# Copying two low-rank products out of their banks, and a later due time for one stage of a chain

## The chip, the core and the metric

The kernel runs on one core of one Trainium2 chip. The metric is the device time of one execution in microseconds. A core has a matrix engine (TensorE, PE in the profile, with its weight loads as PEld), VectorE (DVE), ScalarE (ACT), GpSimd (POOL) and SyncE (SP), which here issues most transfers. TensorE writes its results to PSUM, eight banks; the other engines read them there.

## The reference

One decoder block on 272 tokens (16 meta tokens and 256 of the sequence) with a model width of 2048, all in float32:

```
xn = rms(h, n1);  proj = xn @ w_in                 # 2048 x (3520 + 3088 + 4096)
z_rwkv, z_fox, z_gate = split(proj)
z_rwkv = z_rwkv + (shift(z_rwkv) - z_rwkv) * mu    # token shift
r, k, v, wd, ad, gd = split(z_rwkv)                # 3 x 1024, and low rank 96, 96, 256
decay = exp(-exp(-softplus(-(w0 + tanh(wd) @ w2)) - 0.5))
a = sigmoid(a0 + ad @ a2);  g = sigmoid(gd) @ g2
y_a = groupnorm(wkv7_scan(r, decay, k', v, -kk, kk * a)) + bonus, times g   # 16 heads of 64
y_b = fox(z_fox)                                   # attention with a forget gate, 16 heads of 64
merged = sigmoid(gate_a) * (y_a @ w_a) + sigmoid(gate_b) * (y_b @ w_b)
h = h + merged @ w_o
out = h + (silu(gate) * up) @ w_dn                 # gate, up = split(rms(h, n2) @ w_gu), 5632 wide
```

The scan is a recurrence over tokens for each head.

## The kernel before

**Arithmetic.** Every float32 operand of a large product is split into a high part (a ScalarE copy to a rounded type) and a low part (VectorE subtracts the high part). A weight block is 128 x 1024: `wload` (L304 and on) brings `raw` in over SP's queue, ScalarE makes `wh` (L336), VectorE makes `wl` (L337), and TensorE does three products for one (`mm3`, L346 to L349). `raw`, `wh` and `wl` have four buffers each.

**Order of the work.** First come the low-rank products (`lora_jobs`): eight jobs that add up four banks, `lo0` to `lo3`. `lo0` (96 rows, called `pw`) and `lo1` (112 rows, called `pa`: 96 of the second product and 16 of the forget gate) lie in two of the four `main` banks, the two others in `aux` banks. Then for each of four groups g of four heads: `rwkv_jobs(g)` with the products k, v, r (four jobs each, two banks each) and the second low-rank stage (`g`, `sig`, `aa`), `fox_jobs(g)` with q, k, v of the attention (`f`), and two gate jobs (`zg`). The main banks go round, so the first `v` block takes the banks of `lo0` and `lo1` after the first `k` block took the two others. Branch products (`br`), the output product (`wo`) and the FFN (`gt`, `up`, `dn`) follow.

**Background stages.** Small work runs as generators, the streams, between the blocks of large products. A stream yields the planner nanoseconds until its next stage is due. `slot(ns)` is called after the two or three matmuls that a large product makes from one weight tile, with 3n/2.4 for n columns; it moves a planner clock on and starts at most one due stage, or a pair of a "fox" stage and a "chain" stage that together need at most four aux banks. After a stage the clock must pass MIX times the stage's own TensorE time, at least GAP, before the next one. A fox stage waits for a chain stage up to HOLD, 3500. TensorE's order is written out by hand in this way (`manual_schedule` on TensorE); the other engines' and the queues' orders are set when the program is built, by a planner that lets work go when its model has it ready.

**The streams the change touches.** `token_scales` is spawned by the last low-rank job with a delay of SCALES, 2500. It runs the rms matmuls, the root on VectorE (`rsb`, L263 to L272), and then `lora_post`, which reads the products in `lerp` (L468 for `lo0` and `lo1`, L471 for `lo2` and `lo3`) and in L572, where the forget gate's rows of `pa` are read. Its temporaries come from a ring of six tiles (`zt_`, ZB = 6).

`rwkv_bg(g)` is the scan of a group in chunks of 64 tokens. It builds scaled operands (`ar`, `bk`, one buffer each, L751 to L763), the matrices `NK` (`mat`, L786), and the inverse of a unit triangular matrix for each chunk: 32 x 32 blocks are inverted by 31 steps on VectorE (L874, L876), the results go through DRAM into `X` (L881 to L888), and the last blocks of X are made by two small products. The first, `QT` (32 matmuls of 32 x 32), is copied out by ScalarE (L962, two copies); the second, called X12 in the code and shown as X<-X,QT, reads the copies, is copied to X (L970), and the chain of chunks follows (`rhs`, `u`, `s`, `y`, copies L906, L920, L940 to L944). The first step of that chain, for the meta tokens, is interleaved: its `rhs` goes with the stage before QT, its `u` with QT, its `s` with X12. The lines around it:

```
        for h in range(2):
            nc.scalar.activation(QT[dn(h)].rearrange("p i s -> p (i s)"), ps[dn(h), 0:256], AF.Copy)
        next(meta_steps)
        yield Y_QT, ("chain", 2)
        ps = aux_ps(f"X12{g}")
```

This chain of group g runs while the k, v, r blocks of group g + 1 pass on TensorE; for the last group the gate jobs pass.

Of the kernel before, what the change touches and what calls it, by code (L numbers as in the profile page):

```python
# [12 lines left out]
AF = mybir.ActivationFunctionType  # L13
# [10 lines left out]
L = NMETA + T  # L24
# [66 lines left out]
Y_RHS = 1400  # L91
Y_U = 1400
Y_XT = 1400
Y_QT = 1200
Y_GN = 1400
FORGET = 14000
SCALES = 2500
# [3 lines left out]
def hybrid_block(ctx, tc, A, out, dbg=None):  # L101
    nc = tc.nc
# [17 lines left out]
    def aux_ps(name):  # L120
        return psa.tile([P, 512], F32, tag="aux", name=name)
# [12 lines left out]
    for h in range(2):  # L134
        rows = slice(h * HD, (h + 1) * HD)
# [73 lines left out]
    def zt_(name):  # L209
        return rw.tile([P, 274], F32, tag="z", name=name, bufs=ZB)  # L210
# [5 lines left out]
    def vc(name, i=0):  # L216
        c = COLS[name] + i
        return vcol[:, c:c + 1]
# [4 lines left out]
    def xload(i):  # L223
        xs[i] = et(f"xs{i}")
        nc.sync.dma_start(xs[i], A["hT"][:, 2 * i:2 * i + 2, :])
# [16 lines left out]
    def xsplit(i, m):  # L242

        k = 2 * i + m
        src, sc = (xs[i][:, m, :], vc("n1", k)) if k > 0 else (x0[:, :L], x0[:, L:])
        nc.scalar.activation(xh[:, k, :], src, AF.Copy, scale=sc)
        nc.vector.scalar_tensor_tensor(xl[:, k, :], src, sc, xh[:, k, :].bitcast(F32),
                                       op0=ALU.mult, op1=ALU.subtract)

    def squares(i):  # L250

        if i == 0:
            for m, src in enumerate((x0[:, :L], xs[0][:, 1, :])):
                nc.scalar.activation(xsum[:, m, :], src, AF.Square)
            return
        nc.scalar.activation(xs[i], xs[i], AF.Square)
        nc.vector.tensor_tensor(xsum, xsum, xs[i], op=ALU.add)
# [21 lines left out]
    def rstd1():  # L279
        parts = [et(f"{n}1").bitcast(F32R) for n in ("xqh", "xql")]  # L280
        split(*parts, xsum)

        def back():
            ps = aux_ps("rms1")[:, :L]
            for i in range(4):
                nc.tensor.matmul(ps, allones, parts[i % 2][:, i // 2, :], start=i == 0, stop=i == 3)
            ms = zt_("ms1")[:, :L]
            nc.vector.tensor_scalar(ms, ps, 1.0 / D, RMS_EPS, op0=ALU.mult, op1=ALU.add)
            nc.vector.tensor_scalar(epsw, ms, RMS_EPS, None, op0=ALU.mult)
            rt = zt_("rt1")[:, :L]  # L290
            rsqrt_small(None, rsb, ms, rt, None)
        return back
# [53 lines left out]
    def mm3(ps, wh, wl, ah, al, first, last):  # L346
        nc.tensor.matmul(ps, wh, ah, start=first, stop=False)  # L347
        nc.tensor.matmul(ps, wh, al, start=False, stop=False)  # L348
        nc.tensor.matmul(ps, wl, ah, start=False, stop=last)  # L349
# [8 lines left out]
    def spawn(gen, delay):  # L358
        streams.append([clock[0] + delay, gen, None])
# [148 lines left out]
    def lora_jobs():  # L508
        box = []

        def mk(q):
            def load():
                raw = raw0 if q == 0 else wp.tile([P, 1024], F32, tag="raw", name="raw", bufs=RAWB)
                wh = wp.tile([P, WCOLS], F32R, tag="wh", name="wh", bufs=WB)
                wl = wp.tile([P, WCOLS], F32R, tag="wl", name="wl", bufs=WB)
                if q > 0:
                    nc.sync.dma_start(raw[:, :2 * NLO], A["lora"][q])
                if 0 < q < 7:
                    xload(q + 1)
                for k in range(2):  # L520
                    cs = slice(k * NLO, (k + 1) * NLO)
                    if q == 0 and k == 0:
                        nc.vector.tensor_copy(wh[:, cs], raw[:, cs])
                    xsplit(q, k)
                    if q > 0 or k > 0:
                        nc.scalar.activation(wh[:, cs], raw[:, cs], AF.Copy)
                    nc.vector.tensor_tensor(wl[:, cs], raw[:, cs], wh[:, cs].bitcast(F32), op=ALU.subtract)
                squares(q)
                return [t[:, :2 * NLO].rearrange("p (k c) -> p k c", k=2) for t in (wh, wl)]

            def mul(w):
                if q == 0:
                    box.extend((main_ps if i < 2 else aux_ps)(f"lo{i}") for i in range(4))
                pw, pa, pg0, pg1 = box[:4]
                wh, wl = w
                outs = ((pw, 0, 96, 0, L), (pa, 96, 112, 0, L), (pg0, 208, P, 14, T + 2), (pg1, 208 + P, P, 14, T + 2))
                for k in range(2):
                    kt = q * 2 + k
                    if q == 0:

                        for i, (w_, x_) in enumerate(((wh, xh), (wh, xl), (wl, xh))):
                            for ps, c0, m, n0, n in outs:
                                nc.tensor.matmul(ps[:m, :n], w_[:, k, c0:c0 + m], x_[:, kt, n0:n0 + n],
                                                 start=kt == 0 and i == 0, stop=False)
                        continue
                    for ps, c0, m, n0, n in outs:
                        mm3(ps[:m, :n], wh[:, k, c0:c0 + m], wl[:, k, c0:c0 + m],
                            xh[:, kt, n0:n0 + n], xl[:, kt, n0:n0 + n], False, kt == KT - 1)
                if q == 6:
                    box.append(rstd1())  # L550
                if q == 7:
                    nc.vector.tensor_scalar(qk8, vc("q_g"), vc("k_g"), HD ** -0.5, op0=ALU.mult, op1=ALU.mult)
                    spawn(token_scales(*box), SCALES)
            return load, mul
        return [mk(q) for q in range(8)]

    def token_scales(pw, pa, pg0, pg1, back):
        back()
        lora_post(pw, pa, pg0, pg1)
        spawn(forget_gate(), FORGET)  # L560
        return
        yield

    def lora_post(pw, pa, pg0, pg1):
        tw = zt_("tw")
        lerp(pw, 96, vc("mu_w")[:96], tw[:96, :L], True)
        nc.scalar.activation(tw[:96, :L], tw[:96, :L], AF.Tanh)
        split(twh, twl, tw[:96, :L])
        ad = zt_("ad")
        lerp(pa, 96, vc("mu_a")[:96], ad[:96, :L], True)  # L570
        split(adh, adl, ad[:96, :L])
        nc.vector.tensor_tensor(fl[flr, :], pa[flr, :L], rsb[flr], op=ALU.mult)  # L572
        nc.vector.tensor_scalar(fl[flr, :], fl[flr, :], vc("mu_a")[flr], None, op0=ALU.add)
        for i, pg in enumerate((pg0, pg1)):
            sg = zt_("sg")
            lerp(pg, P, vc("mu_g", i), sg[:, :T], False)
            nc.scalar.activation(sg[:, :T], sg[:, :T], AF.Sigmoid)
            split(sgh[:, i, :], sgl[:, i, :], sg[:, :T])
# [135 lines left out]
    def rwkv_bg(g, box):  # L714
# [248 lines left out]
# [3 lines that stand above are left out]
# [477 lines left out]
```

## Time and profile before

| | us |
|---|---|
| median of 3 runs | 1539.01 |
| lowest and highest | 1537.67 and 1539.15 |
| the profiled execution | 1540.85 |
| its span, from the first to the last instruction | 1539.1 |
| PE busy in the span | 1529.6 (99%) |
| DVE busy | 1030.4 (67%) |
| ACT busy | 778.2 (51%) |
| POOL busy | 106.8 (7%) |

The profile is of one execution. A row of a timeline gives the start and the duration in us, the engine, the line of the kernel, the operation, what is written and read, and, in brackets, the idle time of the engine before it with what ended it. A row of a wait says which engine waited at which line for which work: us in total, times, the longest. A stretch gives each engine's busy us, the number of instructions, the granted clock of TensorE (1.00 is full speed), the DMA engines' share and GB/s. Ends of matmuls are modelled and they overlap, so what counts is the distance from start to start.

### The profile page before, as it was taken

The page shows a single profiled execution, that of the slowest core. Times are in us where ns is not written, and L with a number is a line of the kernel's source. Part 1 is how long each engine was busy: PE and PEld are TensorE (multiplying, and loading weights), DVE is VectorE, ACT ScalarE, POOL GpSimd, SP SyncE. Part 2 cuts the span into 40 slices and gives each one's busy share as a digit, 9 for nine tenths or more (in the row PEclk, how much of TensorE's full clock was granted, in tenths as well). Part 3 has the DMA queues.
Part 4 walks back from the last instruction along what each step waited for, and adds up shares of the span by engine and source line. Part 5 has one row for each costly group of instructions (what it writes and reads, how often), then busy time and mean ns, then how long its engine had stood idle before and what let it go on. Part 6 is the DMA issues. An engine that isn't in the chain of part 4 may idle for free.

```text
span 1539.1 us, 25987 instructions
## 1 busy us (share of the span) xinstructions
PE 1529.6 (99%) x10113; PEld 1352.5 (88%) x10113; DVE 1030.4 (67%) x1859; ACT 778.2 (51%) x1174; POOL 106.8 (7%) x186
## 2 busy tenths in 40 slices
PE   9999999999999999999999999999999999999998
PEld 9999899989989888998888888888888888888887
DVE  7887698688788857876565566666556666444443
ACT  7654465475465445554455455445445544333332
POOL 2111203302202000000000000000000000000000
PEclk9999999999999999999999999999999999999999
DMA  8566546546645757777566666666666665566663
GB/s 269 163 171 185 148 134 188 163 119 188 175 125 154 212 155 218 230 226 240 181 180 185 192 185 186 191 192 182 189 191 191 182 190 189 191 204 204 189 203 104
DMA packets 211483, 283.32 MB, mean 184 GB/s; under 512 B 23888, under 2 KB 128352, under 8 KB 211360
## 3 DMA queue, kind: packets, MB, share of 16 engines
q1 hardware_dynamic: 206752, 277.53, 60.7%
q10 hardware_dynamic: 4608, 4.13, 0.8%
q8 instruction: 79, 1.29, 0.3%
q14 instruction: 44, 0.36, 0.1%
HBM read 274.43 MB, written 7.19 MB: 183 GB/s over the span
## 4 chain that ended last, share of the span: by engine, by line
PE 95%; DVE 2%; ACT 1%; DMA 1%; SPq 1%; issue 1%; DVEq 0%; ACTq 0%
PE up L423 11%; PE gt L423 10%; PE zg L423 8%; PE dn L1306 5%; PE dn L1305 5%; PE dn L1304 5%; PE up L425 5%; PE gt L425 5%; PE zg L425 4%; PE f L347 2%; PE f L349 2%; PE f L348 2%; PE br L347 2%; PE f L423 2%; PE br L348 2%; PE br L349 2%
## 5 line engine op out<-in xcount | busy, mean ns | idle before, releaser
L337 DVE TENSOR_TENSOR wl<-raw,wh 128x1024 fp32r<-128x1024 f32 (+1 forms) x376 | 456.7, 1216 | 264.0 <-ACT wh L336 263.4
L336 ACT ACTIVATE wh<-raw 128x1024 fp32r<-128x1024 f32 (+1 forms) x376 | 393.9, 1049 | 424.8 <-PE up L423 117.5
L318 DVE TENSOR_TENSOR wl<-raw,wh 128x1024 fp32r<-128x1024 f32 x120 | 147.0, 1225 | 162.8 <-ACT wh L317 162.7
L423 PE MATMUL gt<-hts,wh 128*128 128x512 f32 x704 | 245.0, 394 | 0.0
L423 PE MATMUL up<-hts,wh 128*128 128x512 f32 x704 | 244.9, 394 | 0.0
L317 ACT ACTIVATE wh<-raw 128x1024 fp32r<-128x1024 f32 x120 | 127.0, 1058 | 194.4 <-PE dn L1305 141.5
L425 PE MATMUL gt<-hts,wl 128*128 128x256 f32 x660 | 186.2, 282 | 0.0
L425 PE MATMUL up<-hts,wl 128*128 128x256 f32 x660 | 186.0, 282 | 0.0
L423 PE MATMUL zg<-xhl,wh 128*128 128x512 f32 x512 | 182.4, 401 | 0.0
L423 PEld LDWEIGHTS up<-hts,wh 128*128 128x128 f32 x704 | 130.1, 188 | 26.5
L423 PEld LDWEIGHTS gt<-hts,wh 128*128 128x128 f32 x704 | 130.1, 188 | 26.5
L1305 PE MATMUL dn<-wh,acl 128*128 128x512 f32 x352 | 138.7, 394 | 0.0
L1306 PE MATMUL dn<-wl,ach 128*128 128x512 f32 x352 | 138.3, 393 | 0.0
L1304 PE MATMUL dn<-wh,ach 128*128 128x512 f32 x352 | 138.1, 392 | 0.0
L425 PE MATMUL zg<-xhl,wl 128*128 128x256 f32 x480 | 135.0, 281 | 0.0
L425 PEld LDWEIGHTS up<-hts,wl 128*128 128x128 f32 x660 | 124.7, 189 | 1.8
L425 PEld LDWEIGHTS gt<-hts,wl 128*128 128x128 f32 x660 | 124.7, 189 | 1.8
L423 PEld LDWEIGHTS zg<-xhl,wh 128*128 128x128 f32 x512 | 94.3, 188 | 19.4 <-issue 0.7
L425 PEld LDWEIGHTS zg<-xhl,wl 128*128 128x128 f32 x480 | 90.6, 189 | 1.2
L1304 PEld LDWEIGHTS dn<-wh,ach 128*128 128x128 f32 x352 | 66.0, 188 | 15.7
L1305 PEld LDWEIGHTS dn<-wh,acl 128*128 128x128 f32 x352 | 66.1, 188 | 15.4
L1306 PEld LDWEIGHTS dn<-wl,ach 128*128 128x128 f32 x352 | 66.1, 188 | 14.7
(464 smaller groups left out, 2937.9 us busy)
## 6 DMA issues: line engine op xcount, KB each, us to landing
raw<-in_w_gate_up_dram SPq DMA_DIRECT2D x176, 512.0 KB, 3.7
raw<-in_w_in_dram SPq DMA_DIRECT2D x160, 512.0 KB, 4.1
raw<-in_w_down_dram SPq DMA_DIRECT2D x88, 512.0 KB, 4.8
raw<-in_w_o_dram SPq DMA_DIRECT2D x32, 512.0 KB, 4.1
raw<-in_w_branch_a_dram SPq DMA_DIRECT2D x16, 512.0 KB, 4.6
raw<-in_w_branch_b_dram SPq DMA_DIRECT2D x16, 512.0 KB, 4.7
zgd<-zg ACTq DMA_DIRECT2D x30, 128.0 KB, 1.7
gate<-zgd SPq DMA_DIRECT2D x15, 256.0 KB, 6.0
```

The costliest lines, as they stand in the source:

```text
L317: nc.scalar.activation(th, rr, AF.Copy)
L318: nc.vector.tensor_tensor(tl, rr, th.bitcast(F32), op=ALU.subtract)
L336: nc.scalar.activation(wh[:prow, cs_], raw[:prow, cs_], AF.Copy)
L337: nc.vector.tensor_tensor(wl[:prow, cs_], raw[:prow, cs_], wh[:prow, cs_].bitcast(F32), op=ALU.subtract)
L347: nc.tensor.matmul(ps, wh, ah, start=first, stop=False)
L348: nc.tensor.matmul(ps, wh, al, start=False, stop=False)
L349: nc.tensor.matmul(ps, wl, ah, start=False, stop=last)
L423: nc.tensor.matmul(ps.rearrange("p (a t) -> p a t", a=2), wh, act, start=first, stop=last)
L425: nc.tensor.matmul(ps[:, :T], wl, act[:, 0, :], start=False, stop=False)
L1304: nc.tensor.matmul(o, ah[:, kt, ts_], hi, start=first, stop=False)
L1305: nc.tensor.matmul(o, al[:, kt, ts_], hi, start=False, stop=False)
L1306: nc.tensor.matmul(o, ah[:, kt, ts_], lo_, start=False, stop=last)
```

## The change

The planner time between the QT stage and the X12 stage of the inverse, Y_QT, goes from 1200 to 2900, in all four groups. And at the end of the last low-rank job ScalarE copies `lo0` (96 x 272) and `lo1` (112 x 272) into two tiles of the six-tile ring; `token_scales` and `lora_post` get these tiles in place of the banks.

```diff
-Y_QT = 1200
+Y_QT = 2900
...
                 if q == 7:
                     nc.vector.tensor_scalar(qk8, vc("q_g"), vc("k_g"), HD ** -0.5, op0=ALU.mult, op1=ALU.mult)
+                    for i, rows in enumerate((96, 112)):
+                        z = zt_(f"p{i}")
+                        nc.scalar.activation(z[:rows, :L], box[i][:rows, :L], AF.Copy)
+                        box[i] = z
                     spawn(token_scales(*box), SCALES)
```

## The prediction

> **What bounds the kernel now.** I read the page's busy shares first, then the waits of TensorE (PE), then the timeline around each wait, and last the clock by stretches.
>
> ```profile
> span 1539.1 us, 25987 instructions
> PE 1529.6 (99%) x10113; PEld 1352.5 (88%) x10113; DVE 1030.4 (67%) x1859; ACT 778.2 (51%) x1174; POOL 106.8 (7%) x186
> PE X L373 <- ACT QT L962: 2.0, 4, 1.5
> ...
> PE v L347 <- DVE fl L572: 1.1, 1, 1.1
> PE v L347 <- DVE z L468: 0.8, 1, 0.8
> ```
>
> PE is busy for all but 9.5 us, so only what stops or slows PE counts. Its waits inside the kernel are the two that the change touches: `v` waits for VectorE (DVE) to read the low-rank products out of their banks (1.9 us), and the stage of the inverse's last blocks (writing X from QT) waits for ScalarE's (ACT) copies of QT (2.0 us). The gain cannot be much more than these two and what hangs on them.
>
> **Part 1, the copies.** The first `v` block takes the two main banks in which lo0 and lo1 lie. The timeline of PE:
>
> ```profile
> 41.78 0.29 PE L349 MATMUL k<-xhl,wl 128*128 128x272 f32 x1
> 42.84 0.36 PE L347 MATMUL v<-xhl,wh 128*128 128x272 f32 x1 [0.77 <-DVE z L468]
> ...
> 44.29 0.29 PE L349 MATMUL v<-xhl,wl 128*128 128x272 f32 x1
> 45.68 0.36 PE L347 MATMUL v<-xhl,wh 128*128 128x272 f32 x1 [1.10 <-DVE fl L572]
> ```
>
> Where nothing waits, matmuls of about this shape start 0.12 us apart (five steps from 164.41 to 165.02, shown in part 2). The two gaps are 1.06 and 1.39 us from start to start, so they cost 0.94 + 1.27 = 2.2 us over that step. With the copies the banks are free once ACT has read them. What ACT does there:
>
> ```profile
> 29.24 0.29 PE L349 MATMUL lo<-xhl,wl 128*128 128x258 f32 x1
> 29.25 0.64 ACT L490 ACTIVATE xqh<-xsum 128x544 fp32r<-128x544 f32 x1
> 30.71 1.06 ACT L336 ACTIVATE wh<-raw 128x1024 fp32r<-128x1024 f32 x1 [0.82 <-DMA raw<-in_w_in_dram]
> 46.96 0.43 ACT L490 ACTIVATE adh<-ad 96x272 fp32r<-96x272 f32 x1 [1.33 <-DVE ad L479]
> ```
>
> A copy of this size is nearest to the 0.43 us row, two are 0.86. They wait for the last lo matmul (29.53) and fit into ACT's idle 0.82 us behind xqh. Queued behind them stand xqh at worst and the next wh. With both copies ahead of it xqh would end near 31.0 and its DVE partner, which starts at 30.98 now, would hardly move. Were the copies put ahead of the two wh before xqh as well, about 3 us would be pushed and the rms matmuls would wait some 1.5 us. So the price is 0 to 1.5 us. I take 0, since xqh, emitted a job earlier, already stands behind two wh of later jobs: ACT's order follows readiness, not emission. The reads of lo0 and lo1 on DVE stay, now from SBUF, and I leave their durations. The temporaries' ring has two of its six places taken until then.
>
> PE then runs 2.2 us ahead of a DVE that has no slack here, so the next banks decide how much is kept:
>
> ```profile
> 36.00:56.00 20.00, 18.13 (x143) 17.75 (x142) 19.51 (x38) 11.84 (x16) 2.27 (x4) 1.00 0.54 160
> 56.00:68.00 12.00, 12.00 (x100) 11.87 (x98) 10.34 (x15) 6.76 (x9) 2.23 (x6) 1.00 0.60 166
> ...
> 54.78 0.43 DVE L468 TENSOR_TENSOR z<-k,rsb 128x272 f32<-128x272 f32 x1
> 57.75 0.29 PE L347 MATMUL r<-xhl,wh 128*128 128x258 f32 x1
> 70.80 0.39 DVE L689 COPY gg<-g 128x256 f32<-128x256 f32 x1
> 71.55 0.40 PE L423 MATMUL f<-xhl,wh 128*128 128x512 f32 x1
> ```
>
> The first two rows are stretches of 20 and 12 us (busy us of PE, PEld, DVE, ACT, POOL, then clock and DMA): DVE is busy 19.51 of 20. The second half of `r` (57.75) takes a `k` bank that DVE frees at 55.21. PE would come at 55.55: it just fits. The first `f` (71.55) takes the bank that gg frees at 71.19, and would come at 69.35. DVE's work between is released by PE and moves along only as far as DVE has idle time from 56 on (12 - 10.34 = 1.7 us of the 2.2). So some 0.4 us comes back as a new wait (bounds 0 to 2.2). Part 1 is worth 2.2 - 0.4 = 1.8 us.
>
> **Part 2, the later stage.** The same place in groups 0, 1 and 2:
>
> ```profile
> 164.41 0.29 PE L347 MATMUL r<-xhl,wh 128*128 128x258 f32 x1
> ...
> 165.02 0.28 PE L349 MATMUL r<-xhl,wl 128*128 128x258 f32 x1
> 166.83 0.24 PE L373 MATMUL X<-X,QT 32*32 32x32 f32 x2 [1.53 <-ACT QT L962]
> ...
> 167.85 0.45 PE L373 MATMUL s0-1_2290<-SV,BK 128*64 128x64 f32 x8
> ...
> 290.74 0.28 PE L349 MATMUL r<-xhl,wl 128*128 128x258 f32 x1
> 292.23 0.45 PE L373 MATMUL s1-1_3963<-SV,BK 128*64 128x64 f32 x8
> ...
> 413.10 0.28 PE L349 MATMUL r<-xhl,wl 128*128 128x258 f32 x1
> 413.93 0.45 PE L373 MATMUL s2-1_5630<-SV,BK 128*64 128x64 f32 x8
> ```
>
> From the last r matmul to the s matmuls it takes 2.83, 1.49 and 0.83 us; group 2 has no wait. The waits cost 2.0 and 0.66 us; group 3 shows none. QT is late because of ACT's queue:
>
> ```profile
> 158.96 0.97 SPq L332 DMA_DIRECT2D raw<-in_w_in_dram  x2
> 163.14 1.06 ACT L336 ACTIVATE wh<-raw 128x1024 fp32r<-128x1024 f32 x1 [3.19 <-DMA raw<-in_w_in_dram]
> 166.40 0.78 ACT L962 ACTIVATE QT<-QT 32x256 f32<-32x256 f32 x2
> 290.78 0.78 ACT L962 ACTIVATE QT<-QT 32x256 f32<-32x256 f32 x2
> ```
>
> A weight block issued behind the inverse's own transfers lands late, wh waits 3.19 us for it, four Exps and the QT copies stand behind. The stage falls due Y_QT planner nanoseconds after QT's, counted in slots of 3n/2.4: two v slots of 340 and two r slots of 322.5 reach 1325, past 1200. For 2900 seven r slots are needed: nine slots, five more. A slot is three matmuls of 0.122 us (164.41 to 165.02 is five steps), so the stage comes 1.83 us later, at about 167.05. The QT copies end at 167.18, so 0.2 us of waiting is left: gain 1.8 us. In group 1 the stage moves from 291 to past 292.4, the copies end at 291.56: gain 0.66.
>
> Nothing is added to PE. Everything behind in the chain, and the fox stage that is paired with it, moves five slots. The pairing holds, in planner ns from the score stage: QT's stage falls at 1700 (five slots of 340 past 1400), the new stage at 1700 + 2937 = 4637, the chain's next at 4637 + 3050 = 7687; the fox stage is due at 2702 + 2600 = 5302 and waits for a mate until 5302 + 3500 = 8802. Next late in line is `ar`, of which there is one buffer:
>
> ```profile
> 215.08 0.71 DVE L751 SCALAR_TENSOR_TENSOR ar<-k,sig 128x544 f32<-128x544 f32 x1
> 218.34 0.18 DVE L761 TENSOR_TENSOR bk<-k,cs 128x32 f32<-128x32 f32 x1
> L373 PE MATMUL mat<-ar,bk x40: 219/272/373, 223.2 to 233.3; 64*128 64x128 f32 x32, 64*80 64x16 f32 x8
> ```
>
> The new group's `ar` is written once the old chain has read its last; `mat` needs what is ready at 218.52 only at 223.2. Of 4.7 us cover 1.8 are used: cost 0.
>
> **The clock.** In stretches (columns as above, the clock behind POOL):
>
> ```profile
> 165.00:169.00 4.00, 2.31 (x49) 1.88 (x48) 3.84 (x13) 3.89 (x11) 1.21 (x2) 1.00 1.04 341
> 169.00:173.00 4.00, 4.00 (x23) 4.00 (x22) 2.67 (x4) 1.20 (x3) 3.45 (x5) 0.57 0.26 55
> 408.00:420.00 12.00, 12.00 (x166) 11.04 (x163) 9.24 (x31) 7.02 (x19) 6.24 (x9) 1.00 0.89 245
> ...
> 169.29 0.39 PE L349 MATMUL r<-xhl,wl 128*128 128x258 f32 x1
> ...
> 172.71 0.30 PE L347 MATMUL r<-xhl,wh 128*128 128x258 f32 x1
> ```
>
> Right after group 0's wait the granted clock is 0.57 for 4 us, PE busy only 2.31 of the 4 us before. It is the one drop I found; group 2, with the same small matmuls and no wait, stays at 1.00. From 169.29 to 172.71 sixteen matmuls start 0.214 us apart in place of 0.122: 1.5 us lost. Without the wait I expect no drop.
>
> The Trainium skill (TensorE: Matmul & The Clock Gate, Part 1) says that the clock falls back only after an idle window of about 3.4 us, which would clear a 1.5 us wait of blame. The drop here follows a shorter one, so the trace does not agree with the rule as written; by it the sum would be 1.5 us smaller (first rival).
>
> **Sum.** 1.8 + 1.8 + 0.7 + 1.5 = 5.8 us; I take off 0.2, a guess, for small new waits where the later stages fall on other slots: 5.6. The profiled execution took 1540.85 us with its span of 1539.1; it becomes 1535.2 and 1533.5. The runs' median, 1539.01, lies 1.8 under that execution, so 1533.4.
>
> **Rivals.**
> The clock drops anyway, since what triggers it is the small matmuls and not the wait: 5.6 - 1.5 = 4.1, 1534.9. Group 2 speaks against it, the length of the wait for it. 0.11.
> DVE takes the place of the v wait: ring or queue make it late by 2 us at the k or g banks, and part 1 gives all back: 3.8, 1535.2. DVE's full stretches speak for it; 0.11.
> The late weight block does not come earlier with PE. Then X still waits some 2 us in group 0, with the clock: 1.8 + 0.66, 1536.5. But the inverse's run on DVE ends behind this row, which waited for PE, so it moves with PE. 0.09.
>
> ```profile
> 146.90 1.23 DVE L337 TENSOR_TENSOR wl<-raw,wh 128x1024 fp32r<-128x1024 f32 x1 [0.24 <-PE k L349]
> ```
>
> The change doesn't do what it says, `v` waiting on something else and the stage landing in another queue on ACT: about 1539. 0.07.
> Slower: the chain slips more than its five slots because it loses a pairing or a bank, and `mat` waits in groups 1 to 3. It begins at a slip of 4.7 us; with 1.5 us of clock for each wait it decides from about 6.1. At 7 us it costs 3 x (2.3 + 1.5) = 11.4, less 5.6: +5.8, 1544.8. The hold arithmetic speaks against it, the many stages that move for it. 0.12.
>
> **Numbers.** Forecast 0.50, its own range 1532.3 to 1534.8. From the cases: faster (by over 0.2%, 3.1 us, about what a measurement of this kernel can tell) 0.50 + 0.11 + 0.11 = 0.72; same 0.16; slower 0.12. The range goes down to both parts without any give-back (6.4 us) and some noise, 1532.0, and up past the no-change case, 1539.5; the slower case and little else is left out.
>
> **What would show it.** Right: no wait of v behind DVE and v's first matmul 0.13 us after k's last; two ACT copies near 30 us; no more than 0.3 us of waiting of X on QT; clock 1.00 throughout; the f behind g waiting a few tenths. Wrong: a clock near 0.57 somewhere (first rival), PE waits on `z` or gg over 1 us (second), X still waiting over 1 us in group 0 (third), PE waits at `mat` (slower).

## The result: slower by 0.2%, and the profile after

| | before | after |
|---|---|---|
| median of 9 runs each, us | 1538.17 | 1541.36 |
| lowest and highest | 1536.83 and 1539.15 | 1539.71 and 1544.82 |
| the profiled execution | 1540.85 | 1544.82 |

The ratio is 1.0022, with a 95% interval of 1.0012 to 1.0031: slower by 1.9 to 4.8 us. The forecast was 1533.4, faster. The changed kernel's lines from L550 on are numbered four higher (L962 is L966, L920 is L924).

The head of the page of after:

```profile
span 1543.1 us, 25998 instructions
PE 1532.7 (99%) x10113; PEld 1355.8 (88%) x10113; DVE 1030.4 (67%) x1859; ACT 777.2 (50%) x1176; POOL 102.1 (7%) x186
```

TensorE's waits in after (who waited for whom: us in total, times, longest):

```profile
PE X L373 <- DVE SV L924: 2.8, 1, 2.8
PE y L373 <- DVE sv L924: 1.7, 1, 1.7
...
PE f L423 <- ACT aa L701: 0.2, 1, 0.2
```

All waits that the change was to remove are gone: v behind DVE, and X behind QT. Two others stand in their place, each once, and both for the same DVE line, the copy of `u` into `SV`. The two places that the prediction spoke of, in the timeline of after:

```profile
29.84 0.65 ACT L555 ACTIVATE p<-lo 96x272 f32<-96x272 f32 x2
...
41.82 0.29 PE L349 MATMUL k<-xhl,wl 128*128 128x272 f32 x1
41.95 0.29 PE L347 MATMUL v<-xhl,wh 128*128 128x272 f32 x1
...
69.58 0.47 PE L423 MATMUL f<-xhl,wh 128*128 128x512 f32 x1 [0.16 <-ACT aa L701]
...
164.95 0.28 PE L349 MATMUL r<-xhl,wl 128*128 128x258 f32 x1
165.16 0.77 PE L373 MATMUL X<-X,QT 32*32 32x32 f32 x32
165.86 0.45 PE L373 MATMUL s0-1_2309<-SV,BK 128*64 128x64 f32 x8
```

The two copies stand where they were expected, `v` follows `k` after 0.13 us, and X of group 0 follows the last `r` after 0.21 us. So where does the time go? The start of the same blocks in the timelines tells it (a second trace of each kernel is in the two columns on the right):

| first matmul of | before | after | before, second | after, second |
|---|---|---|---|---|
| v, group 0 | 42.84 | 41.95 | 42.06 | 42.16 |
| r, group 0 | 56.30 | 54.00 | 55.48 | 54.22 |
| f, group 0 | 71.55 | 69.58 | 70.73 | 69.47 |
| k, group 1 | 137.64 | 135.75 | 136.82 | 135.54 |
| k, group 2 | 262.66 | 257.43 | 261.90 | 257.14 |
| k, group 3 | 385.02 | 388.91 | 383.60 | 385.42 |
| br | 613.72 | 617.69 | 612.32 | 614.20 |

Until group 2's k blocks the changed kernel is ahead by 5.2 us in the first pair of traces (4.8 in the second). Then comes the stretch in which group 1's chain runs beside group 2's k, v and r: it takes 131.5 us in place of 122.4 (128.3 in place of 121.7). From there on nothing changes: 228.8 against 228.7 us to the branch products. The whole loss is in that one stretch. Its start, in the timeline of after:

```profile
281.74 0.36 SPq L1104 DMA_DIRECT2D bias<-ncd  x1
...
284.34 0.78 DVE L468 TENSOR_TENSOR z<-v,rsb 128x272 f32<-128x272 f32 x2
...
285.00 0.45 PE L373 MATMUL u1-1_3938<-R1-1_3884,X 64*64 64x64 f32 x8
...
286.42 0.91 POOL L1107 TENSOR_SCALAR b<-bias,cq,hs 128x144 f32<-128x144 f32 x2 [6.46 <-DMA bias<-ncd]
...
289.62 0.28 PE L349 MATMUL r<-xhl,wl 128*128 128x258 f32 x1
...
289.77 0.65 POOL L476 TENSOR_TENSOR zd<-z 128x272 f32<-128x272 f32 x1
...
290.46 0.50 DVE L479 SCALAR_TENSOR_TENSOR v<-zd,vcol,z 128x272 f32<-128x272 f32 x1 [5.34 <-POOL z L467]
...
291.92 0.57 DVE L924 COPY SV<-u1-1_3938 16x128 f32<-16x128 f32 x2
...
292.74 1.15 PE L373 MATMUL X<-X,QT 32*32 32x32 f32 x32 [2.84 <-DVE SV L924]
```

Read it from the end. X is put 2.84 us late by DVE's copies, though `u` was ready at 285.4. (X does not read SV. In the program as built its product goes into the PSUM bank in which this `u` lies, so the bank has to be copied out first; the `s` products right behind it read SV.) The copies stand in DVE's queue behind `v` (L479), which needs POOL's `zd`. `z` was there at 285.1, but POOL makes `zd` only at 289.77: ahead of it in POOL's queue stands the attention's bias (L1107), whose transfer was issued at 281.74 and let POOL go on at 286.42. In the timeline of before the transfer of this bias was issued at 287.78, and POOL's bias comes behind both `zd`:

```profile
288.21 0.64 POOL L476 TENSOR_TENSOR zd<-z 128x272 f32<-128x272 f32 x1 [2.80 <-DVE nm L1129]
...
289.86 0.59 DVE L920 COPY SV<-u1-1_3890 16x128 f32<-16x128 f32 x2
...
291.07 0.82 POOL L476 TENSOR_TENSOR zd<-z 128x272 f32<-128x272 f32 x1 [2.17 <-DVE sums L1139]
292.22 1.20 POOL L1103 TENSOR_SCALAR b<-bias,cq,hs 128x144 f32<-128x144 f32 x2 [0.33 <-DMA bias<-ncd]
```

The second wait, in the timeline of after:

```profile
338.48 0.45 PE L373 MATMUL u<-R,X 64*64 64x64 f32 x8
...
338.98 0.28 DVE L924 COPY sv<-u 64x128 f32<-64x128 f32 x1 [0.34 <-PE u L373]
...
339.25 0.71 DVE L755 SCALAR_TENSOR_TENSOR ar<-k,sig 128x544 f32<-128x544 f32 x1
...
342.39 0.47 DVE L773 SCALAR_TENSOR_TENSOR rk<-r,vcol,kf 128x256 f32<-128x256 f32 x1
342.89 0.29 DVE L924 COPY sv<-u 64x128 f32<-64x128 f32 x1
...
343.23 0.45 PE L373 MATMUL y<-sv,NK 128*64 128x64 f32 x6 [1.73 <-DVE sv L924]
```

The two halves of `u` are copied one after the other before (338.42 and 338.80 in the first trace of before); now the next group's `ar`, `k`, `rk` and `bk` stand between them, 3.6 us of DVE work. The stretches around both waits (busy us of PE, PEld, DVE, ACT, POOL, then the granted clock and DMA):

```profile
289.15:292.56 3.41, 0.75 (x7) 0.54 (x5) 1.55 (x5) 3.09 (x9) 2.31 (x5) 1.00 0.69 221
292.56:299.39 6.83, 6.65 (x63) 6.50 (x64) 4.21 (x7) 1.81 (x3) 0.31 (x1) 0.50 0.53 156
299.39:302.80 3.41, 3.41 (x39) 2.73 (x39) 0.35 (x2) 0.66 (x2) 0.00 (x0) 1.00 0.52 153
340.35:343.76 3.41, 1.68 (x17) 1.32 (x16) 3.38 (x9) 1.41 (x3) 0.00 (x0) 1.00 0.33 115
343.76:347.17 3.41, 3.41 (x16) 3.41 (x17) 2.97 (x6) 1.42 (x5) 0.00 (x0) 0.50 0.46 128
```

Behind each wait the granted clock is 0.50, for 6.83 us and for 3.41 us: 10.24 us at half speed, 5.1 us lost. That is as much as the difference between the profiled execution and the fastest runs of after (1544.82 and 1539.7), whose mean granted clock is 1.000.

### The profile page after: what moved, and what is told of

Read it like the earlier page. It is cut to its first block, busy times and chain, and to the rows that moved or that the text cites. A ratio compares the mean times of both kernels' runs of the same rounds, so it can differ in the third digit from the quotient of the medians.

```text
span 1543.1 us, 25998 instructions
## 1 busy us (share of the span) xinstructions
PE 1532.7 (99%) x10113; PEld 1355.8 (88%) x10113; DVE 1030.4 (67%) x1859; ACT 777.2 (50%) x1176; POOL 102.1 (7%) x186
## 4 chain that ended last, share of the span: by engine, by line
PE 95%; DVE 2%; DMA 1%; SPq 1%; issue 0%; ACT 0%; POOL 0%; DVEq 0%; ACTq 0%; POOLq 0%
PE up L423 11%; PE gt L423 10%; PE zg L423 7%; PE dn L1309 5%; PE dn L1310 5%; PE dn L1308 5%; PE up L425 5%; PE gt L425 5%; PE zg L425 3%; PE f L347 2%; PE f L349 2%; PE f L348 2%; PE br L347 2%; PE br L348 2%; PE f L423 2%; PE br L349 2%
```

## The experiments

Theory A, formed from these rows: group 0's chain ends later, and by that the attention of group 1 (its "fox" stages) loses the pairing with group 1's chain; its bias work goes ahead on POOL, and DVE's copy comes late. The planner's rule in `slot` is

```
if mate and mate[0][0] > clock[0] and clock[0] < st[0] + HOLD and mate[0][0] < st[0] + HOLD:
    continue
```

that is, a fox stage waits only for a chain stage that is due within HOLD, 3500, of its own due time. In the planner's clock, as the kernel counts it when it is built, group 1 stands like this:

```
                                            before    after
last step of group 1's inverse              164640   165920
its chain's first stage due (LANE, 24000)   188640   189920
group 1's bias issued                       155360   155040
its score stage due (BIAS, 30000)           185360   185040
the score stage holds if the chain's
due time is under (HOLD, 3500)              188860   188540
```

Before, the pairing held by 220 planner ns. After, the old chain's last stages take slots in the gate jobs that the new group's had; the inverse comes 1280 later, the bias 320 earlier, and the score stage goes alone. In group 3 the pairing is lost in the same way (due at 359040 against 357660, where before it was 357760 against 357980), and nothing waits there: beside the last group's chain the gate jobs pass, not a next group's `v`, and POOL's rows show no `zd` in that stretch. So a lost pairing costs nothing by itself; it costs where POOL's `zd` stand behind the bias.

### Each part alone

```diff
-Y_QT = 2900
+Y_QT = 1200
```

> The two ScalarE copies alone, Y_QT at 1200 as before. Theory A (the loss in group 1 comes from the later stage: the chain of group 0 ends later, group 1's fox stage loses its pairing, POOL's bias work goes ahead of zd, and DVE's copy of u to SV comes late): no new wait of X on SV and none of y; the 1.9 us of part 1 that the trace of after shows at the first f (71.55 to 69.58) stay to the end, so about 1.9 below the kernel before: 1536.3 against 1538.2; X still waits some 2 us on QT in group 0, with a clock drop in some executions. Rival B (the lead of 1.9 us that the copies give is what upsets DVE and POOL in group 1): the wait of X on SV of 2.8 us is there, and the time is 1540 or more.

Measured: 1536.89 against 1538.15, ratio 0.9995 (0.9986 to 1.0004). No wait on SV or sv in its trace; X waits 1.4 us for QT in three places, 1.07 of it in group 0. Theory A stands and rival B falls, but of the 1.9 us the median shows 1.3, and the interval includes no change at all.

The second has Y_QT 2900 and not the copies:

> Y_QT at 2900 in all groups, without the copies. Theory A: the same lost pairing in group 1 as after the whole change, X waits on SV by 2 to 3 us there and y by up to 2 us; the time is that of the whole change plus the 1.9 us of the copies: 1543.3 against 1541.4. Rival B: without the lead of the copies no wait of X on SV; the stage gives its 1.8 + 0.66 and the clock: about 1534 to 1536.

Measured: 1543.01, ratio 1.0033 (1.0021 to 1.0044). X waits 2.2 us and y 1.7 us in group 1, with DVE idle 5.17 us for POOL ahead of `v` as above. The view puts X's wait down to ScalarE's `wh` there; but DVE's copies end at 293.11, 0.25 us ahead of X, the same distance as in after, and in the program X waits for these copies and not for `wh`. So the later stage alone makes the loss, and the copies take 1.3 and 1.6 us off, without and with it.

### The lost pairing

```diff
-HOLD = 3500
+HOLD = 7000
```

> The whole change, and HOLD from 3500 to 7000, so that the fox stage of groups 1 and 3 waits for its chain stage again (in the kernel before the same HOLD changes no instruction on any engine). The bias work of POOL then stands behind four zd again. Theory A: no wait of X on SV in group 1, the lead of 5.2 us at the k blocks of group 1 (262.66 to 257.43) is kept past X and s, 2.8 us and the clock drop of 292 to 300 (some 2 us) are gone: 1535 to 1537 if the wait of y (1.7) stays in some form, 1533 to 1534 if not. Rival C (X placed nine slots behind QT meets DVE's late SV copy whatever the pairing): the wait stays at 2 to 3 us and the time at 1540 to 1542.

Measured: 1537.99 (1537.60 to 1539.17), ratio 0.9999 (0.9990 to 1.0008); 3.4 us under the whole change. The waits of this kernel and where two of them lie:

```profile
PE pv L377 <- ACT ya L1003: 2.1, 2, 1.0
...
PE pvm L377 <- ACT bt L847: 0.7, 2, 0.3
```

```profile
357.94 0.60 PE L377 MATMUL yT<-ident,Y 128*128 128x128 f32 x4
...
358.73 0.60 PE L377 MATMUL trbk<-ident,bk 128*128 128x128 f32 x4
...
360.01 0.28 PE L377 MATMUL pvm<-ident,vv 128*16 128x128 f32 x1 [0.33 <-ACT bt L847]
361.34 0.44 PE L377 MATMUL pv<-ident,vv 128*128 128x128 f32 x2 [1.04 <-ACT ya L1003]
```

The waits on SV and sv are gone, so theory A holds on the cause and rival C falls. The time it named does not hold: with y's wait gone it was 1533 to 1534, 4 to 5 us too low. 2.8 us of that are new waits. The chain now ends later still, and its last transpose `yT` falls between the two `trbk`, right ahead of the attention's `pv`, which waits until ScalarE has read a bank: 1.4 us in each of two groups. A later stage finds a new neighbour. The rest was not traced.

```diff
-        yield Y_QT, ("chain", 2)
+        yield (Y_QT if g else 1200), ("chain", 2)
```

> The whole change, but group 0 keeps Y_QT 1200; groups 1, 2 and 3 have 2900. Theory A: group 0's chain ends where it did before, so group 1's fox stage keeps its pairing: no wait of X on SV in group 1 although its own stage is later. What stays is group 0's wait on QT (2.0) with its clock drop: gain 1.9 of the copies and 0.66 of group 1's wait, about 1535.7 to 1536.5. Rival C: X waits on SV in group 1 by 2 to 3 us, 1539 to 1541.

Measured: 1536.26, ratio 0.9988 (0.9979 to 0.9997), as theory A had it. The waits:

```profile
PE X L373 <- ACT QT L966: 1.0, 2, 0.8
```

Both of these waits lie in group 0 (0.83 us and 0.16). Group 1's own stage is five slots later here and nothing waits in group 1. What costs the time in group 1 was done in group 0. (Group 3's pairing is lost here too, by the same numbers as above, and nothing waits in group 3.) The counterpart, Y_QT 2900 in group 0 alone (`g == 0`):

> The whole change, but only group 0 has Y_QT 2900; groups 1 to 3 keep 1200. Theory A (group 0's later end alone loses group 1's pairing, and the SV copy is late there whenever X comes): X of group 1 comes five slots, 1.8 us, earlier and the copy does not, so the wait grows from 2.8 to 4 to 4.6 us; the last y of group 1's chain comes where it did before and does not wait; sum about that of the whole change, 1540.5 to 1542.5. Rival E (the later stage of group 1 itself makes the wait): no wait on SV in group 1, part 1 and group 0's gains are kept: 1533 to 1535.

Measured: 1541.35, ratio 1.0018 (1.0009 to 1.0027). The waits:

```profile
PE X L373 <- DVE SV L924: 4.3, 1, 4.3
```

X comes earlier and the copy does not, so the wait grows as theory A counted, by 1.4 us; y does not wait. Rival E (1533 to 1535) falls. The wait of y thus needs both, the lost pairing and group 1's own later stage: neither of these two kernels has it.

### The queue of DVE

```diff
-                nc.vector.tensor_copy(SV[0:nt, h, mine, :], pv2(ps)[h * HD:h * HD + nt])
+                nc.scalar.activation(SV[0:nt, h, mine, :], pv2(ps)[h * HD:h * HD + nt], AF.Copy)
```

> The whole change, and the copies of u into SV are made by ScalarE in place of DVE, in every step of the chain; the order of the stages is that of the whole change, with the pairing lost. Theory A (X and y wait because DVE's queue is held: by v behind POOL's late zd in the one place, by the next group's ar and bk in the other): in ScalarE's queue the copy stands right behind the QT copies, which end at 290.2, so it would end near 290.8; X, which comes at 289.9, waits about 1 us in place of 2.8, and y does not wait. About 3.5 us less than the whole change, and less clock to lose: 1537 to 1538. Rival D (X waits for something else that comes at the same time, QT or the bank): X still waits 2 us or more, 1540 to 1541.

Measured: 1535.92 (1535.12 to 1537.79), ratio 0.9985 (0.9976 to 0.9994): the lowest median of all, 5.4 us under the whole change and 1 to 2 us under what was expected (its interval overlaps those of the two kernels at 1536.3). Its waits, without warmup and lo:

```profile
PE f L423 <- DVE eps L614: 0.6, 1, 0.6
```

Neither X nor y waits, with the pairing still lost and the bias still ahead of `zd` (DVE is idle 4.93 us for POOL, and nobody cares). X waits less than the 1 us expected: it starts at 290.07, right behind the QT copies, and the SV copy ends at 290.59, in time for the s matmuls at 290.69. X can go ahead of the SV copy because the program has given it another bank here, that of QT in place of that of `u`; so this edit moved a copy and, with it, a bank. Is it the change or the place of the copies that is worth this? The same edit without either part, and with the low-rank copies alone:

> The kernel before, with the copies of u into SV made by ScalarE as in the run that was fastest so far (1535.9); neither part of the change. Theory A: the kernel before has no wait on SV, so the place of the copies is worth nothing by itself: 1537.7 to 1538.7. Rival G: ScalarE's copies shorten the chain or free DVE in all groups, and the 1535.9 comes from them and not from the two parts: 1536 or less.

> The two copies of the low-rank products and the SV copies on ScalarE, but Y_QT 1200. Beside the run with all three (1535.9) it tells what the later stage is worth when nothing waits on SV. Theory A: X waits for QT in group 0 by 1.0 to 1.4 with a clock drop in some executions: 1536.5 to 1537.2, so the later stage is worth about 1 us in the median. Rival: 1536 or less, the later stage is worth nothing.

Measured: 1538.05 (ratio 0.9998, 0.9989 to 1.0008) and 1536.76 (0.9990, 0.9981 to 0.9999), both as theory A had it. The SV copies are worth nothing where DVE does not hold them. Once their side effect is out of the way, the two parts of the change together take 2.3 us off the median (1535.92 against 1538.19, clear of the noise). How that divides is less sure: 1.3 us for the low-rank copies is just clear of it here (it is not in the first experiment), 0.8 us for the later stage is not.

One link was taken out alone: the two `zd` of the `v` that passes during group 1's chain, made by DVE:

```diff
-        if later is None:
+        if later is None or on_dve:
             nc.vector.tensor_tensor(d[:rows, :n], pr, cu, op=ALU.subtract)
...
-                    lerp(pss[m], P, mc, ..., full, box["done"])
+                    lerp(pss[m], P, mc, ..., full, box["done"], nm == "v" and g == 2)
```

> The whole change, with the lost pairing, but the two zd of group 2's v (the blocks that pass during group 1's chain) are made by DVE, not by POOL, so that DVE does not wait for POOL there. Theory A: DVE's idle 5.3 us in front of v is gone, its copy of u to SV is done before X comes, X waits no more than 0.3; the wait of y (1.7) stays: 2.8 us and one of the two clock drops less than the whole change, 1537 to 1538.5. Rival D (POOL's late zd is not what holds the copy): X waits 2 us or more and the time is within 1 us of 1541.4.

Measured: 1539.85, ratio 1.0011 (1.0002 to 1.0020), 1.5 us under the whole change; X waits 1.1 us in place of 2.8 (listed under `wh` again, 0.26 us behind the end of DVE's copies), y 1.7 as in the whole change. More than the expected 0.3 is left. DVE's rows say why:

```profile
289.54 0.44 DVE L474 TENSOR_TENSOR zd<-z 128x272 f32<-128x272 f32 x1 [3.49 <-POOL z L467]
...
290.43 0.57 DVE L924 COPY SV<-u1-1_3938 16x128 f32<-16x128 f32 x2
```

POOL also clears the first column of `z` (L467), 0.1 us of work, and that was left in its queue behind the bias. The copy comes 1.5 us earlier, X waits 1.7 us less: the link is POOL, and only part of it was cut.

### A smaller step in group 0

```diff
-        yield Y_QT, ("chain", 2)
+        yield (1900 if g == 0 else Y_QT), ("chain", 2)
```

> The whole change, but group 0 has Y_QT 1900 (two slots later than before, in place of five), the others 2900: group 0's chain then ends early enough for group 1's pairing. Theory A: no wait on SV; X of group 0 waits 0.1 to 0.3 us on QT in place of the 1.0 that is left with 1200 there, so 0.7 us less than that kernel's 1536.3, and fewer clock drops: 1535.0 to 1535.8, which is under both kernels. Rival: a loss of pairing or a new wait elsewhere, 1537 or more.

Measured: 1536.28, ratio 0.9988 (0.9979 to 0.9997). X of group 0 waits 0.4 us in place of 1.0 and the pairing holds, but the median is that of the kernel with 1200 there; the expected 0.7 us is not seen. Its trace has a wait of `f` of 0.4 us that the other's has not.

### A second trace of each

> The kernel before once more, for a second trace. The prediction's sum was made against one execution of 1540.85, and the median of the runs is now 1538.2. Theory F: that execution held more of the very waits that the sum counts than most do. Then here X waits for QT in group 0 by 1.0 to 1.3 in place of 1.5, v for DVE by 1.5 in place of 1.9, the clock has no drop after X or a shorter one, and the br products start at 610 to 612 in place of 613.72. Rival H: the waits are of the same size in every execution, and what differs lies elsewhere (the first 30 us, transfers).

It took 1539.42. Its waits, without warmup and lo:

```profile
PE X L373 <- ACT QT L962: 1.8, 2, 1.6
...
PE v L347 <- DVE fl L572: 1.1, 1, 1.1
```

X's wait in group 0 is as long as before and has a clock drop behind it again (rival H there). But `v` waits once, not twice, and X of group 1 does not wait (theory F there): 1.6 us of what the sum counted (0.94 for `z`, 0.66 for group 1) is not in every execution.

> The whole change once more, for a second trace. The order on every engine is fixed, so the waits of X on SV (2.8) and of y on sv (1.7) are there again within 0.5 us; the clock drops behind them are not fixed: with none the execution takes about 1539.7, with one 1541.5, with two 1544. Rival I: in an execution without clock drops the waits are not there either, that is, drop and wait come together.

It took 1541.34. Its waits and stretches:

```profile
PE X L373 <- DVE SV L924: 2.5, 1, 2.5
PE y L373 <- DVE sv L924: 1.7, 1, 1.7
```

```profile
289.90:293.31 3.41, 1.22 (x41) 1.14 (x42) 2.86 (x6) 1.83 (x5) 0.92 (x2) 1.00 0.18 57
293.31:296.73 3.42, 3.42 (x17) 3.42 (x18) 1.73 (x5) 1.27 (x3) 0.31 (x1) 0.50 0.68 188
...
337.68:341.10 3.42, 1.90 (x16) 1.61 (x14) 3.39 (x10) 1.14 (x2) 0.00 (x0) 1.00 0.48 147
341.10:344.51 3.41, 3.21 (x28) 3.14 (x29) 3.38 (x7) 2.70 (x6) 0.00 (x0) 1.00 0.27 71
```

The waits are there again, one drop of 3.41 us follows the first, none the second. Rival I falls: the waits belong to the order of the work, the drops are added or not.

## Why the prediction was wrong, point by point

**Part 1** was right. `v` does not wait, the lead is 2.30 us at the first `r`, 1.97 at the first `f` and 1.89 at group 1's k, against a forecast of 2.2 and, after a give-back, 1.8. The give-back shows as forecast, as a wait of `f` of 0.2 us here and 0.3 to 0.6 in three of the experiments (in the program `f` waits there for the copy `gg`; the views name a neighbour, `aa` or `eps`). Only the 0.94 us for the wait on `z` is not in every execution: in the second pair of traces the lead at the same three places is 1.3 us, and 1.3 us is what the median of the copies alone shows.

**Part 2 in group 0** was right in the traces. From group 1's k to group 2's k it is 121.7 us in place of 125.0: 3.3 us, the 1.8 of the wait and the 1.5 of the clock.

**The failed step** is "Nothing is added to PE. Everything behind in the chain, and the fox stage that is paired with it, moves five slots. The pairing holds". The arithmetic was right for the pair it was made for, inside a chain. It was not made for the pair with which the next group's chain begins; that one held by 220 planner ns, and the change moved it by 1600. So "The pairing holds" was false in groups 1 and 3, and "Nothing is added to PE" was false in group 1: in place of a gain of 0.66 it has two waits, 2.84 and 1.73 us in the first trace. In the second pair of traces its stretch is 6.6 us longer; 4.2 of that are the waits, 1.7 the clock (3.41 us at half speed), and 0.7 I could not place.

**`ar`** was named as late next, with 4.7 us of cover to `mat`. `mat` does not wait. But `ar` and what follows it fill DVE's queue, and a copy that the old chain's last `y` needs got behind them: only the readers of `ar` had been looked at, not who shares its engine.

**The clock**: "Without the wait I expect no drop" was right in group 0, where the drop is gone. "Clock 1.00 throughout" was wrong, since the new waits have drops of their own. And the 1.5 us were a gain for some executions only: of the 80 runs of before beside the experiments, 40 have a mean granted clock of 1.000, so no such drop (median 1537.4), and 17 read 0.998 (median 1538.8).

**From the execution to the median**: the sum was made against an execution of 1540.85 and the 1.8 us between it and the median taken off at the end. What set that execution apart was in part what the sum had counted as gain: the two waits that are not in every execution (1.6 us together), and the drop. The kernel in which neither `v` nor X nor y waits any more, the one with the SV copies on ScalarE, has its median at 1535.9, not at 1533.4.

So of the 8.0 us between 1533.4 and 1541.4, 5.4 went away with the SV copies moved to ScalarE (1541.4 to 1535.9), an edit that is worth nothing in the kernel before: they are the two waits and the drops behind them. The other 2.5 are the sum's: waits and a drop of one execution, taken off a median that holds them only in part.

**The rivals.** The slower one named a lost pairing as the cause, and was right in that; it put the wait at `mat` in three groups from a slip of 4.7 us on. The pairing was lost in two groups, from a slip of 220 planner ns, and the waits came in one, at X and y.

## What to carry to other kernels

When a stage is moved by a planner's delay, work out every later "due within" rule of the planner, also for the next group, in its own clock: the margin there was 220 planner ns, and it can be read from the planner's clock when the kernel is built, before anything is run. A wait of one engine is paid where two queues cross: here a copy of 0.6 us stood behind an operation that waited for GpSimd, and with that copy on ScalarE the whole change gains 2.3 us (1535.9 against 1538.2 before). And where a median stands well under the profiled execution, ask whether the difference is the very wait that is to be removed.

## What the hardware did that I had not expected

In these traces the granted clock in a drop is 0.50, a drop lasts 3.41 us or twice that, and in one execution the drops begin on a common grid: in the first trace of after at 292.56 and 343.76, fifteen times 3.413 us apart. The granted clock of 0.57 that the prediction read was a stretch that held some full speed too. In the two traces of after each drop begins at the end of a 3.41 us stretch of that grid in which TensorE was busy for 0.75, 1.22 or 1.68 us. A stretch with 1.90 us of 3.42 was followed by none. That fits with the same wait of y, 1.73 us, costing 1.7 us more in one execution and nothing more in the other, by how it lies on the grid; two traces do not prove it.

The Trainium skill (TensorE: Matmul & The Clock Gate, Part 1) has such a free-running window of about 3.4 us, and the length and the grid agree with it; its condition, an idle window, does not: half of a window was enough here, and a wait of 1.73 us. The prediction had noted that disagreement; what it lacked was the grid. What the threshold is stays open, and busy time in the profile alone does not decide it. Two stretches of the same grid in the first trace of before:

```profile
43.02:46.43 3.41, 2.31 (x18) 2.12 (x18) 3.25 (x7) 0.88 (x3) 0.00 (x0) 1.00 0.73 217
165.90:169.31 3.41, 2.32 (x49) 2.10 (x50) 3.28 (x12) 3.04 (x7) 1.21 (x2) 1.00 0.95 317
```

Behind the first, 18 matmuls of the large shape, the clock stays at 1.00; behind the second, 49 matmuls, many of them 32 x 32, comes the drop. That would fit with small matmuls counting for less than their rows' length; no run here tests it.

The runs fit in the main, as far as their mean granted clock tells. One drop alone reads as 0.998 or 0.999, and so can the last microseconds of a span (with 1200 in group 0 the trace has its only drop from 1532.5 us on, and reads 0.999), so a count of 0.998 or less is the least there can be. It was that in 8 of 10 runs of the kernel with the 4.3 us wait, in 3 of 9 of the whole change, 3 of 6 with the later stage alone, 17 of 80 of the kernel before (1.5 us), 2 of 10 each with waits of 1.1 and 1.7 us and with the SV copies alone moved (1.6 us), 1 of 10 with both kinds of copies (1.3 us), 2 of 11 with the low-rank copies alone (1.07 us), 1 of 11 with 1200 in group 0 (0.83 us), and in none of 32 runs of the other three (HOLD, the SV copies on ScalarE, the smaller step), whose longest wait in the middle of the span was 1.04 us.
